# A tail of 232 matmuls in thirteen forms and 29 VectorE and GpSimd operations, added behind the output of a two-layer decoder

## The chip, the cores and the metric

The kernel runs on one NeuronCore of a Trainium2 chip. The metric is the device time of one execution in microseconds (us). Names of engines are those of the profile: PE is TensorE's matmul stream, PEld its weight loads, DVE is VectorE, ACT is ScalarE, POOL is GpSimd, SP is SyncE, which issues the loads.

## The reference

Two layers are applied to a residual `h` of 256 tokens by 1024 channels. All arithmetic is float32, and the output is the last residual.

```python
for i in range(DEPTH):                       # DEPTH = 2
    xn = rms_norm(h, norm_mix[i])
    u = xn @ w_in[i]                         # split into the inputs of four mixers
    branches = (o_a, o_b, o_c, o_d)          # RG-LRU, conformer, differential, sparse attention
    mixed = sum(sigmoid(xn @ w_gate[i, j]) * (branches[j] @ w_branch[i, j]) for j in range(4))
    h = h + mixed @ w_out[i]
    f = causal_dwconv(rms_norm(h, norm_ffn[i]) @ w_up[i], conv_f_w[i], conv_f_b[i])
    f_gate, f_val = jnp.split(f, 2, axis=-1)
    h = h + (jax.nn.silu(f_gate) * f_val) @ w_down[i]
    e = rms_norm(p[i] @ w_ple_in[i], ple_norm[i])
    g = sigmoid(rms_norm(h, ple_gate_norm[i]) @ w_ple_gate[i])
    h = h + g * e
return h
```

## The kernel before

The channels lie in the partitions and the tokens in the columns. The residual is four tiles `h[0]` to `h[3]` of 128 by 512 (two blocks of 128 channels, 256 tokens each). The weights come as a stream of pieces of 128 by 1024 float32. `prep_one` (line 205) loads a piece into `raw`, ACT writes its high part `hi` (line 214, type float32r) and DVE the remainder `lo` (line 215). A product is three matmuls on such parts, in `mm3` (lines 248 to 250): high by high, high by low, low by high. A matmul there takes 128 rows of contraction, a stationary operand of 128 columns and a moving operand of 256 columns. `tok_unit` (lines 476 to 478) does the same with moving operands of 512 columns. Side computations of the mixers use plain float32 matmuls: the RG-LRU gates at lines 794 and 796 (128 rows, 256 columns), the scores of the differential attention at line 703 (64 rows, because a head has 64 channels), each followed by a bfloat16 matmul on 128 rows at line 704 that adds the mask, and the sums of squares at line 271, with a moving operand of one column. In the trace a float32 matmul leaves two records on PE, one of float32r or bfloat16 a single record.

Each engine runs its instructions in the order of its own queue, and semaphores order them between engines. That order comes from a scheduler that follows the program and the dependences of the tiles. Tiles come from pools with a fixed number of buffers: `big` (38), `raw` (5), `hi` (6) and, in PSUM, `mm` and `sp` (4 banks each; `smbank` gives one `sp` bank).

The program ends with the last layer's gate. For each `h[i]`, PE computes the gate's product, DVE scales it (line 1038), ACT takes the tanh (line 1039), DVE multiplies and adds (lines 1040 and 1041), and ACT issues the DMA of that part of `h[i]` to the output (line 1043). `h[3]` is done in two halves of 256 columns. POOL does nothing but four memsets at the program's start.

Of the kernel before, what the change touches and what calls it, by code (L numbers as in the profile page):

```python
# [10 lines left out]
F32 = mybir.dt.float32  # L11
F32R = mybir.dt.float32r
# [6 lines left out]
P = 128  # L19
# [8 lines left out]
NEG = -1e30  # L28
THETA = 500000.0
PIECE = 1024  # L30
EARLY = 4  # feed-forward banks computed before the mean square is known
MIX = (0, 3, 2, 1)
MIX_ORDER = (("gate", MIX[0]), ("gate", MIX[1]), ("branch", MIX[0]), ("gate", MIX[2]), ("branch", MIX[1]),
             ("gate", MIX[3]), ("branch", MIX[2]), ("branch", MIX[3]))
# how far apart the steps of the side computations lie between the products: RG-LRU, conformer,
# differential attention, sparse attention, first half of the conformer's taps
EVERY = {0: 4.8, 1: 5.1, 2: 3.3, 3: 2.9, 4: 5.5}

# columns of the channel vectors
_V = {}  # L40
_o = 0
for _n, _w in (("norm_mix", 8), ("norm_ffn", 8), ("ple_gate_norm", 8), ("ple_norm", 8), ("conv_a_w", 16),
# [3 lines left out]
    _o += _w  # L46
NV = _o

# columns of the row vectors
_R = {}  # L50
_o = 0
for _n, _w in (("diff_q_norm", 64), ("diff_k_norm", 64), ("diff_lq1", 64), ("diff_lk1", 64), ("diff_lq2", 64),
# [2 lines left out]
    _o += _w  # L55
NR = _o

# columns of the shape-only constants
_C = {}
_o = 0  # L60
for _n, _w in (("ident", 128), ("nc30", 128), ("nc38", 128), ("rope_c", 64), ("rope_s", 128), ("rope_i", 32), ("hmask", 4)):
# [3 lines left out]


def unit_list(l):
    """One layer's weights in the order of their use: (key, source, pieces), a piece being
    (first k-tile, k-tiles, column ranges or counts of zero columns)."""
    u = []  # L70

    def tok(key, c0, c1, src="w_in", kt=KD):
        g = PIECE // (c1 - c0)
        u.append((key, src, [(k, g, [(c0, c1)]) for k in range(0, kt, g)]))

    def chan(key, src, c0, kt=KD, g=8):
        u.append((key, src, [(k, min(g, kt - k), [(c0, c0 + P)]) for k in range(0, kt, g)]))

    def bu(n):
        chan(("bv", n), "w_in", 1024 + n * P)  # L80
        chan(("bg", n), "w_in", 1536 + n * P)

    ple_in = [(("ple_in", i), "w_ple_in", [(0, 2, [(512 * i, 512 * i + 512)])]) for i in range(2)]
    if l:
        u.append(ple_in[0])
    for n in range(4):
        bu(n)
    if not l:
        u.append(ple_in[0])
    tok(("tok", "dq"), 3584, 4096)  # L90
    tok(("tok", "dk"), 4096, 4608)
    u.append((("ik", 0), "w_in", [(0, KD, [(4608, 4648), P - 40])]))
    tok(("tok", "cq"), 2048, 2560)
    tok(("tok", "ck"), 2560, 3072)
    tok(("tok", "cv"), 3072, 3584)
    for n in range(8):
        chan(("a", n), "w_in", n * P)
    for kind, j in MIX_ORDER:
        if kind == "gate":
            for n in range(8):  # L100
                chan(("gate", j, n), ("w_gate", j), n * P)
        else:
            for n in range(0, 8, 2):
                tok(("branch", j, n), n * P, (n + 2) * P, ("w_branch", j), 4)
    u.append(ple_in[1])
    for n in range(8):
        chan(("out", n), "w_out", n * P)
    for g in range(NG):
        chan(("upg", g), "w_up", g * P)
        chan(("upv", g), "w_up", D_FF + g * P)  # L110
    for n in range(8):
        chan(("down", n), "w_down", n * P, NG)
    for n in range(8):
        chan(("pg", n), "w_ple_gate", n * P)
    return u
# [7 lines left out]
def decoder_kernel(ctx: ExitStack, tc: tile.TileContext, w_dram, x_dram, p_dram, vec_dram, row_dram, lru_dram,  # L123
# [28 lines left out]
        return ps.tile([P, 4, P], F32, name=nm("sp"), tag="sp", bufs=4)  # L152

    def score_banks(Kw):
        """Banks for four maps [P, Kw]: (maps of the bank, bank [P, maps, Kw])."""
        n = 2 * S // Kw
        return [(range(i, i + n), smbank().rearrange("p a b -> p (a b)").rearrange("p (a b) -> p a b", a=n))
                for i in range(0, 4, n)]

# [1 line left out]
    h = [cst.tile([P, 2, S], F32, name=f"h{i}", tag=f"h{i}") for i in range(4)]  # L161
    con = cst.tile([P, NC], F32, name="con", tag="con")
    vec = [cst.tile([P, NV], F32, name=f"vec{l}", tag=f"vec{l}") for l in range(L)]
# [16 lines left out]
    mask_bf = cst.tile([P, 2, P], BF16, name="mask_bf", tag="mask_bf")  # L180
    ident_bf, nc30_bf = mask_bf[:, 0, :], mask_bf[:, 1, :]

    # the tensor engine's clock rises with activity: keep it busy until the first operands are there
    warm = smbank()
    for _ in range(12):
        T.matmul(warm[:, 0, :], ones, ones, start=True, stop=True)

# [1 line left out]
    stream = []  # L189
    pidx = 0  # L190
    for l in range(L):
# [34 lines left out]
        used[0] += npieces  # L226
        return r

# [1 line left out]
    def split(dst, src, scale=1.0):  # L230
        """dst = (hi, lo) from src, exactly."""
        hi, lo = dst
        if scale == 1.0:
            A.activation(hi, src, AF.Copy)  # L234
            V.tensor_tensor(lo, src, hi.bitcast(F32), op=ALU.subtract)  # L235
        else:
            A.activation(hi, src, AF.Copy, scale=scale)
            V.scalar_tensor_tensor(lo, src, scale, hi.bitcast(F32), op0=ALU.mult, op1=ALU.subtract)

    def mm3(out, wl, xs, c0, first, last):  # L240
        """out += W[:, c0:c0+128].T @ x over the piece's k-tiles."""
        wh, wlo = wl
        nk = len(xs)
        for k in range(nk):
            xh, xl = xs[k]
            a = wh[:, k, c0:c0 + P]
            b = wlo[:, k, c0:c0 + P]
            T.matmul(out, a, xh, start=first and k == 0, stop=False)  # L248
            T.matmul(out, a, xl, start=False, stop=False)  # L249
            T.matmul(out, b, xh, start=False, stop=last and k == nk - 1)  # L250
# [13 lines left out]
        V.tensor_tensor(acc[:, 0, :], acc[:, 0, :], acc[:, 1, :], op=ALU.add)  # L264

    def rnorm(acc, scale, bias):
        """1 / sqrt(scale * (sum over the channels) + bias) per token: with the tokens in
        partitions [P, 2], and in every partition [P, S]."""
        t = smbank()
        for b in range(2):  # L270
            T.matmul(t[:, 0, b:b + 1], acc[:, 0, b * P:(b + 1) * P], ones[:, 0:1], start=True, stop=True)  # L271
        rt = st([P, 2], "rt", 4)
        A.activation(rt, t[:, 0, 0:2], AF.Sqrt, scale=scale, bias=bias)
        V.reciprocal(rt, rt)
        t = smbank()
        for b in range(2):
            T.matmul(t[:, b, :], rt[:, b:b + 1].to_broadcast([P, P]), ident, start=True, stop=True)  # L277
        rs = st([P, S], "rs", 3)
        A.activation(rs, t[:, 0:2, :].rearrange("p a b -> p (a b)"), AF.Copy)
        return rt, rs  # L280

    class Norm:
        """RMSNorm over all channels of [128, 2, S] pairs. xs: split x * gain, for products whose
        result is scaled by r afterwards; xn(): split x * gain * r."""

        def __init__(self, gain, late=False):
            self.gain, self.late, self.pairs, self.xs, self.acc, self.squares = gain, late, [], [], None, 0
# [46 lines left out]
            return t  # L334

    def rope(t, H, W, tab, b):
        """t [128, H, W]: rotates the first W/4 columns of each head."""
        rot = W // 4
        half = rot // 2
        q = t[:, :, 0:rot]  # L340
        cs = tab[:, b, 0, :][:, None, :].to_broadcast([P, H, rot])
        sn = tab[:, b, 1, :]
        t1 = st([P, P], "rp1", 2)[:, :H * rot].rearrange("p (h r) -> p h r", h=H)
        t2 = st([P, P], "rp2", 2)[:, :H * rot].rearrange("p (h r) -> p h r", h=H)
        V.tensor_tensor(t1, q, cs, op=ALU.mult)
        V.tensor_tensor(t2[:, :, 0:half], q[:, :, half:rot], sn[:, None, 0:half].to_broadcast([P, H, half]), op=ALU.mult)
        V.tensor_tensor(t2[:, :, half:rot], q[:, :, 0:half], sn[:, None, half:rot].to_broadcast([P, H, half]), op=ALU.mult)
        V.tensor_tensor(q, t1, t2, op=ALU.add)
# [5 lines left out]
        split(hl, pT)  # L354
        return hl

    # ================= layers =================
    for l in range(L):
        vv = vec[l]
        rr = cst.tile([P, NR], F32, name=nm("row"), tag="row")  # L360
# [7 lines left out]
            o, w = _R[name]  # L368
            return rr[:, o:o + w]

# [1 line left out]
        if l == 0:  # L372
            nxt_nrm = Norm(vcol("norm_mix"), late=True)
            for i in range(4):
# [29 lines left out]

        if l:
            embed(0)
# [1 line left out]
        nrm = nxt_nrm  # L408
        xsk = ktiles(nrm.xs)
        bbanks = []  # L410
# [16 lines left out]
            A.activation(ident_bf, ident, AF.Copy)  # L427
            A.activation(nc30_bf, nc30, AF.Copy)

# [1 line left out]
        sv = st([P, 44], "sv", 2)  # L431
        hbr, hbi, lc2, lc4, b2 = (sv[:, 4 * i:4 * i + 4] for i in range(5))
        z, z2, pz, ee = (sv[:, 20 + 4 * i:24 + 4 * i] for i in range(4))
# [29 lines left out]
        hr = nrm.rt  # L463

        def tok_unit(xk, n, npieces):
            """u[:, cols] token-major, one bank per token block."""
            pcs = take(npieces)
            outs = []
            outs = [mmbank().rearrange("p a b -> p (a b)")[:, :n] for b in range(2)]
# [11 lines left out]
            return outs  # L481

        def weave(gens):
            """The steps of the generators in turn."""
            live = list(gens)
            while live:
                for g in list(live):
                    if next(g, "end") == "end":
                        live.remove(g)
                    else:  # L490
                        yield
# [11 lines left out]

        o_pairs = {}

# [1 line left out]
        def side_d():  # L507
            dq, dk, ik = raws["dq"], raws["dk"], raws["ik"]
            ms = st([P, 2, 6], "msd", 1)
# [142 lines left out]

            yield from weave(attend(b) for b in range(2))

# [1 line left out]
        def side_c():  # L656
            cq, ck, cv = raws["cq"], raws["ck"], raws["cv"]
            ms = st([P, 2, 2, 8], "msc", 1)
# [103 lines left out]
                                           op1=ALU.subtract)  # L762
                yield

# [1 line left out]
        xa, ga = [], []  # L766

        def evac_a(bank, i):
# [48 lines left out]
                oa.append(hl)  # L817
                yield

# [1 line left out]
        ypad = st([P, 4, S + 30], "ypad", 1)  # L821
        V.memset(ypad[:, :, 0:30], 0.0)

# [62 lines left out]
                for _ in sides.pop(k)[0]:  # L886
                    pass

# [1 line left out]
        for c in range(4):  # L890
            evac_b(nrm.scaled(bbanks[c]), c)
        if not l:
# [29 lines left out]
                fn(bank, i)  # L922
        side(0, side_a(), EVERY[0])

# [1 line left out]
        mixed = {}  # L926
        gates = {}
        ms_ = []
# [41 lines left out]
            V.scalar_tensor_tensor(h[i], bank, 0.5, h[i], op0=ALU.mult, op1=ALU.add)  # L970
            nrm.add(h[i])

# [1 line left out]
        _, rs = rnorm(acc[0], 4.0 / D, eps[:, 1:2])  # L974
        for i in range(4):
            V.tensor_tensor(e[i], e[i], rs[:, None, :].to_broadcast([P, 2, S]), op=ALU.mult)
# [70 lines left out]
                nxt_nrm.add(h[i])  # L1047


def _rope_rows(head_dim):  # L1050
    rot = head_dim // 4
    inv = np.float32(THETA) ** (-np.arange(0, rot, 2, dtype=np.float32) / np.float32(rot))
# [18 lines left out]


def _chan(a):
    """[C] or [taps, C] -> [128, C/128 * taps]: channel c*128+p at partition p."""
    a = np.asarray(a)
    if a.ndim == 1:
        a = a[None]
# [51 lines left out]
```

## Time and profile before

| | |
|---|---|
| time, median of two runs | 1067.38 us (1066.74 and 1068.01) |
| span of the profiled execution, first to last instruction | 1064.7 us |
| PE busy | 1056.7 us, 99% of the span |
| DVE, ACT busy | 874.1 us, 708.1 us |
| POOL busy | 0.2 us |
| HBM read | 181.21 MB, 171 GB/s over the span |

The page gives the span of the profiled execution and not its time; the two times shown are 2.0 and 3.3 us longer than the span, the median 2.7 us. A busy share says how much of the span an engine had an instruction in hand. Matmuls overlap in the array, so a matmul's price is read from the distance between the starts of two neighbours and not from its length.

### The profile page before, as it was taken

What the parts mean: (1) busy time and instruction counts of PE and PEld (TensorE: products, weight loads), DVE (VectorE), ACT (ScalarE), POOL (GpSimd) and SP (SyncE); (2) the same over time, 40 slices, a digit from 0 to 9 for tenths busy, and PEclk for the clock granted to TensorE, in tenths of its full rate; (3) what the DMA queues carried; (4) which work ended last, traced back from release to release, by engine and by line L of the source; (5) the groups of instructions that cost most, each with busy time, mean ns of one, the idle gap of its engine ahead of it and who ended that gap; (6) DMA issues with size and microseconds to landing.
All of it is one profiled execution on the core that took longest, in us unless ns stands there. A gap on an engine that the chain in (4) does not pass through costs nothing.

```text
span 1064.7 us, 20765 instructions
## 1 busy us (share of the span) xinstructions
PE 1056.7 (99%) x8168; PEld 1018.3 (96%) x8168; DVE 874.1 (82%) x1629; ACT 708.1 (67%) x1207; POOL 0.2 (0%) x4
## 2 busy tenths in 40 slices
PE   8999999999999999999999999999999999999998
PEld 8888999899999999999998899998999999999998
DVE  7999999868888997855787899997779789877554
ACT  7876788668466766544677769876685667665442
POOL 0000000000000000000000000000000000000000
PEclk9999999999999999999999999999999999999999
DMA  8755244434555365555554643443455554655541
GB/s 299 279 188 194 100 142 166 159 131 158 190 182 175 121 237 183 179 188 194 181 187 167 214 163 120 139 171 115 165 169 185 173 181 147 221 177 176 184 161 40
DMA packets 52369, 183.60 MB, mean 172 GB/s; under 512 B 5808, under 2 KB 6320, under 8 KB 52272
## 3 DMA queue, kind: packets, MB, share of 16 engines
q1 hardware_dynamic: 51408, 181.05, 49.9%
q8 instruction: 64, 1.05, 0.4%
q10 hardware_dynamic: 864, 1.24, 0.4%
q14 instruction: 33, 0.27, 0.1%
HBM read 181.21 MB, written 1.05 MB: 171 GB/s over the span
## 4 chain that ended last, share of the span: by engine, by line
PE 98%; DVE 1%; DMA 0%; ACT 0%; issue 0%; DVEq 0%
PE mm L249 27%; PE mm L248 27%; PE mm L250 27%; PE mm L476 3%; PE mm L478 3%; PE mm L477 3%; PE sp L703 2%; PE sp L564 1%; PE sp L625 1%; PE sp L733 1%; PE sp L704 0%; PE sp L648 0%; DMA vec<-in_vec_dram 0%; PE sp L277 0%; PE sp L271 0%; PE sp L683 0%
## 5 line engine op out<-in xcount | busy, mean ns | idle before, releaser
L248 PE MATMUL mm<-b,hi 128*128 128x256 f32 x2384 | 680.5, 286 | 1.9 <-ACT hi L214 1.7
L250 PE MATMUL mm<-b,lo 128*128 128x256 f32 x2384 | 675.6, 284 | 0.2 <-DVE lo L215 0.2
L249 PE MATMUL mm<-b,hi 128*128 128x256 f32 x2384 | 675.8, 284 | 0.0
L214 ACT ACTIVATE hi<-raw 128x1024 fp32r<-128x1024 f32 (+1 forms) x343 | 357.2, 1046 | 259.0 <-PE mm L249 199.0
L215 DVE TENSOR_TENSOR lo<-raw,hi 128x1024 fp32r<-128x1024 f32 (+1 forms) x343 | 411.1, 1204 | 122.8 <-ACT hi L214 120.1
L248 PEld LDWEIGHTS mm<-b,hi 128*128 128x128 f32 x2384 | 457.4, 192 | 3.0 <-ACT hi L214 1.9
L249 PEld LDWEIGHTS mm<-b,hi 128*128 128x128 f32 x2384 | 458.0, 192 | 1.3 <-issue 0.5
L250 PEld LDWEIGHTS mm<-b,lo 128*128 128x128 f32 x2384 | 457.8, 192 | 0.4 <-DVE lo L215 0.4
L840 DVE SCALAR_TENSOR_TENSOR b<-s,vec,b 128x256 f32<-128x256 f32 x240 | 103.6, 476 | 0.0
L476 PE MATMUL mm<-hi,b 128*128 128x512 f32 x160 | 62.9, 393 | 0.0
L478 PE MATMUL mm<-hi,b 128*128 128x512 f32 x160 | 62.5, 390 | 0.0
L477 PE MATMUL mm<-lo,b 128*128 128x512 f32 x160 | 62.4, 390 | 0.0
L1009 DVE SCALAR_TENSOR_TENSOR s<-mm,vec,s 128x255 f32<-128x255 f32 (+1 forms) x144 | 59.8, 474 | 1.7 <-ACT s L1003 1.7
L234 ACT ACTIVATE b<-b 128x512 fp32r<-128x512 f32 x56 | 35.0, 628 | 28.1 <-DVE b L1013 18.4
L235 DVE TENSOR_TENSOR b<-b,b 128x512 fp32r<-128x512 f32 x56 | 38.4, 686 | 12.3 <-ACT b L234 12.3
L478 PEld LDWEIGHTS mm<-hi,b 128*128 128x128 f32 x160 | 30.0, 188 | 6.4
L476 PEld LDWEIGHTS mm<-hi,b 128*128 128x128 f32 x160 | 30.0, 188 | 6.4
L1003 ACT ACTIVATE s<-mm,vec 128x256 f32<-128x256 f32 x72 | 36.1, 551 | 0.0
L477 PEld LDWEIGHTS mm<-lo,b 128*128 128x128 f32 x160 | 30.1, 188 | 5.8
L709 ACT ACTIVATE s<-sp,s,s 128x128 f32<-128x128 f32 (+1 forms) x32 | 16.0, 507 | 12.7 <-DVE s L706 12.7
L295 ACT ACTIVATE b<-h,vec 128x256 fp32r<-128x256 f32 x48 | 21.4, 497 | 2.4 <-DVE h L1041 2.4
L296 DVE SCALAR_TENSOR_TENSOR b<-h,vec,b 128x256 fp32r<-128x256 f32 x48 | 20.8, 478 | 0.8 <-ACT b L295 0.8
(206 smaller groups left out, 792.4 us busy)
## 6 DMA issues: line engine op xcount, KB each, us to landing
raw<-in_w_dram SPq DMA_DIRECT2D x325, 512.0 KB, 3.3
raw<-in_w_dram SPq DMA_DIRECT2D x16, 384.0 KB, 2.9
h<-in_x_dram SPq DMA_DIRECT2D x4, 256.0 KB, 5.1
b<-in_lru_dram SPq DMA_DIRECT2D x4, 256.0 KB, 6.1
out_dram<-h ACTq DMA_DIRECT2D x3, 256.0 KB, 2.5
row<-in_row_dram SPq DMA_DIRECT2D x2, 336.0 KB, 5.6
raw<-in_w_dram SPq DMA_DIRECT2D x2, 256.0 KB, 5.0
b<-in_p_dram SPq DMA_DIRECT2D x2, 256.0 KB, 4.9
```

Of the source, the lines that this page charges most:

```text
L214: A.activation(hi[:, cs], raw[:, cs], AF.Copy)
L215: last_lo[0] = V.tensor_tensor(lo[:, cs], raw[:, cs], hi[:, cs].bitcast(F32), op=ALU.subtract).ins
L235: V.tensor_tensor(lo, src, hi.bitcast(F32), op=ALU.subtract)
L248: T.matmul(out, a, xh, start=first and k == 0, stop=False)
L249: T.matmul(out, a, xl, start=False, stop=False)
L250: T.matmul(out, b, xh, start=False, stop=last and k == nk - 1)
L476: T.matmul(outs[b], xk[k][0][:, bs], wh[:, kk, :], start=k == 0, stop=False)
L477: T.matmul(outs[b], xk[k][0][:, bs], wl[:, kk, :], start=False, stop=False)
L478: T.matmul(outs[b], xk[k][1][:, bs], wh[:, kk, :], start=False, stop=k == last)
L840: V.scalar_tensor_tensor(t, ypad[:, c, d:d + S], w[:, 31 * c + d:31 * c + d + 1], t, op0=ALU.mult, op1=ALU.add)
L1003: A.activation(cf[:, 2 * q + s_, :], bank[:, s_, :], AF.Identity, scale=w[:, 3 * c + 2:3 * c + 3], bias=bb[:, c:c + 1])
L1009: V.scalar_tensor_tensor(t, bank[:, s_, :S - d], w[:, 3 * c + 2 - d:3 * c + 3 - d], t, op0=ALU.mult, op1=ALU.add)
```

## The change

Code is added at the end of `decoder_kernel`, after the loop over the layers. ACT copies `h[0]` to `wide` and `h[3]` to `stat` (both float32r) and `h[3]` to `wbf` (bfloat16). Thirteen calls of `run` then issue 232 matmuls into `sp` banks that nothing reads. `full` uses all 128 rows (or 96 of the stationary columns); `rows` takes 64 or 32 rows at a time, from the partitions of one row group after the other, and writes each row group to its own bank. Beside it ACT copies `h[2]` and `h[3]` into one tile `src` of 128 by 1024, and a chain of 15 DVE and 14 POOL operations of 128 by 1024 runs on it, handing tiles back and forth. No result of the tail goes to the output, and no instruction of the kernel before is taken out. The other changed lines of the diff are comments and docstrings.

```diff
@@ -1047,6 +1047,77 @@
                 nxt_nrm.add(h[i])


+    wide = big.tile([P, 2, S], F32R, name=nm("b"), tag="big", bufs=NBIG)
+    A.activation(wide, h[0], AF.Copy)
+    stat = big.tile([P, 2, S], F32R, name=nm("b"), tag="big", bufs=NBIG)
+    A.activation(stat, h[3], AF.Copy)
+    w32, x32, idn = h[3], h[0], ident
+    wbf = cst.tile([P, 2, S], BF16, name="wbf", tag="wbf")
+    A.activation(wbf, h[3], AF.Copy)
+
+    def flat(bank):
+        return bank.rearrange("p a b -> p (a b)")
+
+    def run(n, make):
+        banks = [smbank() for _ in range(4)]
+        for q in range(n):
+            make(q, [flat(b) for b in banks])
+
+    def full(w, x, N, M=P):
+        def f(q, banks):
+            T.matmul(banks[q % 2][:M, :N], w[:, q % 2, 0:M], x.rearrange("p a b -> p (a b)")[:, :N], start=True, stop=True)
+        return f
+
+    def rows(w, x, N, k):
+        n = P // k
+        def f(q, banks):
+            r = q % n
+            rs = slice(r * k, (r + 1) * k)
+            T.matmul(banks[r][:, :N], w[rs, (q // n) % 2, 0:P], x.rearrange("p a b -> p (a b)")[rs, :N], start=True, stop=True)
+        return f
+
+    run(16, full(stat, wide, 256))
+    run(16, rows(stat, wide, 256, 64))
+    run(16, full(stat, wide, 256))
+    run(32, rows(stat, wide, 256, 32))
+    run(16, full(stat, wide, 512))
+    run(16, rows(stat, wide, 512, 64))
+    run(16, full(stat, wide, 128))
+    run(16, full(stat, wide, 256, 96))
+    run(16, full(wbf, wbf, 256))
+    run(16, rows(wbf, wbf, 256, 64))
+    run(8, full(w32, x32, 256))
+    run(16, rows(w32, x32, 256, 64))
+    run(32, rows(w32, x32, 256, 32))
+
+    src = wp.tile([P, PIECE], F32, name=nm("raw"), tag="raw", bufs=RAW_BUFS)
+    for i in range(2):
+        A.activation(src[:, 512 * i:512 * i + 512].rearrange("p (a b) -> p a b", a=2), h[2 + i], AF.Copy)
+    G = nc.gpsimd
+
+    def tmp(dtype=F32):
+        return wp.tile([P, PIECE], dtype, name=nm("hi"), tag="hi", bufs=SPLIT_BUFS)
+
+    hi = tmp(F32R)
+    V.tensor_copy(hi, src)
+    d = [tmp(F32R) for _ in range(2)]
+    for q in range(2):
+        V.tensor_tensor(d[q], src, hi.bitcast(F32), op=ALU.subtract)
+    g = [tmp(F32R) for _ in range(2)]
+    for q in range(2):
+        G.tensor_tensor(g[q], d[q].bitcast(F32), hi.bitcast(F32), op=ALU.subtract)
+    for q in range(6):
+        V.tensor_tensor(d[q % 2], g[0].bitcast(F32), hi.bitcast(F32), op=ALU.subtract)
+        G.tensor_tensor(g[1], g[0].bitcast(F32), hi.bitcast(F32), op=ALU.subtract)
+    for q in range(3):
+        V.tensor_copy(d[q % 2], g[1].bitcast(F32))
+    for q in range(3):
+        G.tensor_copy(g[0], d[q % 2].bitcast(F32))
+    for q in range(3):
+        V.scalar_tensor_tensor(d[q % 2], g[0].bitcast(F32), 1.0, hi.bitcast(F32), op0=ALU.mult, op1=ALU.subtract)
+        G.tensor_tensor(g[1], g[0].bitcast(F32), hi.bitcast(F32), op=ALU.subtract)
+
+
 def _rope_rows(head_dim):
     rot = head_dim // 4
     inv = np.float32(THETA) ** (-np.arange(0, rot, 2, dtype=np.float32) / np.float32(rot))
```


On ACT, at the program's end, two of the tail's copies are put between the steps of the last gate (`raw` is the tile `src`, `b_13147` is `wide`), and three behind the last output DMA (`b_13149` is `stat`):

```order
 L1043 DMA out_dram<-h_72 128x512
 L1039 ACTIVATE b_13110<-b_13110 128x256
+L1095 ACTIVATE raw_13437<-h_72 128x512
 L1043 DMA out_dram<-h_73 128x256
+L1051 ACTIVATE b_13147<-h_70 128x512
 L1039 ACTIVATE b_13141<-b_13141 128x256
 L1043 DMA out_dram<-h_73 128x256
-L1124 UNCONDITIONAL_BRANCH
+L1053 ACTIVATE b_13149<-h_73 128x512
+L1056 ACTIVATE wbf<-h_73 128x512
+L1095 ACTIVATE raw_13437<-h_73 128x512
```

The copies of `h[2]` and `h[0]` now stand ahead of the last two output DMAs' steps, the copies of `h[3]` behind them.

On POOL, whose rows ended with the branch after the memsets, this stands behind that branch now (`hi_13440` is `hi`, 13442 and 13443 are `d[0]` and `d[1]`, 13446 and 13447 `g[0]` and `g[1]`):

```order
 L1108 ISA
 L1108 TENSOR_TENSOR hi_13446<-hi_13442,hi_13440 128x1024
 L1108 TENSOR_TENSOR hi_13447<-hi_13443,hi_13440 128x1024
 L1111 TENSOR_TENSOR hi_13447<-hi_13446,hi_13440 128x1024 x6
 L1115 CAST hi_13446<-hi_13442 128x1024
 L1115 CAST hi_13446<-hi_13443 128x1024
 L1115 CAST hi_13446<-hi_13442 128x1024
 L1118 TENSOR_TENSOR hi_13447<-hi_13446,hi_13440 128x1024 x3
```

POOL waits there for DVE's `d[0]` and `d[1]`, and DVE's subtractions at line 1110 and casts at line 1113 wait for POOL's results; nothing moved on POOL, all of it is new.

## Rows read from the trace of the kernel before

**Rows 1.** the page: busy time, share of the span, instructions; then the chain's engines

```profile
PE 1056.7 (99%) x8168; PEld 1018.3 (96%) x8168; DVE 874.1 (82%) x1629; ACT 708.1 (67%) x1207; POOL 0.2 (0%) x4
...
PE 98%; DVE 1%; DMA 0%; ACT 0%; issue 0%; DVEq 0%
```

**Rows 2.** timeline of the end: start us, us, engine, line, operation [idle, releaser]

```profile
1059.58 0.28 PE L250 MATMUL mm<-b,lo 128*128 128x256 f32 x1
1059.90 0.42 DVE L1038 TENSOR_TENSOR b<-mm,s 128x256 f32<-128x256 f32 x1 [1.08 <-PE mm L250]
1060.36 0.42 ACT L1039 ACTIVATE b<-b 128x256 f32<-128x256 f32 x1 [2.46 <-DVE b L1038]
...
1061.26 0.42 DVE L1041 TENSOR_TENSOR h<-b,h 128x256 f32<-128x256 f32 x1
1061.72 0.34 ACTq L1043 DMA_DIRECT2D out_dram<-h  x1
```

**Rows 3.** DMA issues of the page: KB each, us from issue to landing

```profile
out_dram<-h ACTq DMA_DIRECT2D x3, 256.0 KB, 2.5
```

**Rows 4.** groups by line and form: xcount, busy us, mean ns, idle us

```profile
L215 DVE TENSOR_TENSOR lo<-raw,hi 128x1024 fp32r<-128x1024 f32 x325 | 394.5, 1219 | 116.4 <-ACT hi L214 114.2
...
L234 ACT ACTIVATE b<-b 128x512 fp32r<-128x512 f32 x56 | 35.0, 628 | 28.1 <-DVE b L1013 18.4 <-DVE b L814 4.0 <-DVE b L955 3.2
...
L812 DVE TENSOR_TENSOR_SCAN b<-b,b 128x256 f32<-128x256 f32 x8 | 5.0, 668 | 0.0
...
L1040 DVE SCALAR_TENSOR_TENSOR b<-b,b 128x512 f32<-128x512 f32 x7 | 4.8, 688 | 2.8 <-ACT b L1039 2.8
...
L348 DVE TENSOR_TENSOR b<-s,s 128x128 f32<-128x128 f32 x12 | 3.4, 281 | 0.0
...
L535 DVE COPY s<-s 128x128 f32<-128x128 f32 x4 | 0.9, 213 | 0.0
```

**Rows 5.** the same view for POOL alone, first of four like rows

```profile
L1117 POOL MEMSET const-bfloat16-1.0<- 128x1 bf16 x1 | 0.1, 101 | 0.0
```

**Rows 6.** timeline of PE, 512-column matmuls of one token unit

```profile
36.58 0.40 PE L476 MATMUL mm<-hi,b 128*128 128x512 f32 x1
36.81 0.40 PE L477 MATMUL mm<-lo,b 128*128 128x512 f32 x1
```

**Rows 7.** chain in order of time: start us, us, what (two float32 matmuls)

```profile
129.59 0.87 PE sp L794 x4
```

**Rows 8.** timeline of PE's weight loads around four one-column matmuls

```profile
1039.87 0.53 PEld L271 LDWEIGHTS sp<-ones,b 128*128 128x128 f32 x4
1040.33 0.19 PEld L249 LDWEIGHTS mm<-b,hi 128*128 128x128 f32 x1
```

**Rows 9.** timeline of PE: float32 on 64 rows beside bfloat16 on 128

```profile
157.39 0.28 PE L249 MATMUL mm<-b,hi 128*128 128x256 f32 x1
157.51 0.28 PE L250 MATMUL mm<-b,lo 128*128 128x256 f32 x1
157.72 0.48 PE L703 MATMUL sp<-b,b 64*128 64x128 f32 x2
158.14 0.23 PE L704 MATMUL sp<-mask_bf 128*128 128x128 bf16 x1
```

**Rows 10.** stretches: busy of PE, PEld, DVE, ACT, POOL; then PEclk, DMA, GB/s

```profile
6.00:7.00 1.00, 0.00 (x0) 0.00 (x0) 1.00 (x3) 1.00 (x3) 0.00 (x0) 1.00 1.07 389
...
9.00:10.00 1.00, 1.00 (x7) 1.00 (x6) 1.00 (x3) 1.00 (x4) 0.00 (x0) 0.50 1.05 428
12.00:14.00 2.00, 2.00 (x19) 2.00 (x18) 1.93 (x5) 1.97 (x6) 0.00 (x0) 0.97 1.03 411
1063.20:1063.40 0.20, 0.00 (x0) 0.00 (x0) 0.00 (x0) 0.00 (x0) 0.00 (x0) 1.00 0.00 0
1063.60:1064.00 0.40, 0.00 (x0) 0.00 (x0) 0.00 (x0) 0.00 (x0) 0.00 (x0) 0.50 0.00 0
```

## The prediction

> **What bounds the kernel now.** I read the page first: PE is busy 99% of the span and makes 98% of the chain that ended last, and POOL is busy 0.2 us [rows 1]. So the kernel is one PE stream, and whatever is put behind it has nothing to hide under, except the few microseconds after the last matmul. These I read from the timeline of the end: the last matmul starts at 1059.58, the last addition to `h[3]` (line 1041) ends at 1061.68, and the last output DMA is issued from 1061.72 to 1062.06 [rows 2]. With 2.5 us to landing [rows 3] the output is complete at about 1064.2 to 1064.6, which is the span of 1064.7. The median time is 2.7 us longer than that span, and I carry these 2.7 us over.
>
> **What starts when.** Nothing is removed, and no step of the old program is put behind an added one for long: two copies of 128 by 512 stand between the last steps on ACT, at 0.63 us each [rows 4]. ACT idles 2.46 us before its last tanh at 1060.36 [rows 2], which covers both copies and the DMA issue between them; uncovered they would cost at most 1.3 us. All the rest needs `h[3]`, which is final at 1061.68. Behind the DMA issue ACT writes `stat` from 1062.06 to 1062.69, then `wbf`, then the second half of `src` until 1062.06 + 3 x 0.63 = 1063.95. Two chains start there and run side by side: PE's from about 1062.8, DVE and POOL's from 1063.95. The later one sets the end. The output's landing, at 1064.6, is hidden under both.
>
> **PE's chain.** The price of a matmul is the distance between starts. For float32r with 256 columns it is 0.12 us [rows 9], with 512 columns 0.23 [rows 6]. A float32 matmul of 128 rows and 256 columns costs 0.87 / 2 = 0.435 (four records are two matmuls) [rows 7]. With one column, four records are still (1040.33 - 1039.87) / 4 = 0.115 apart [rows 8], so a weight load of 128 columns takes about 0.11 however short the matmul is. I take 0.11 for float32r with 128 columns (0.23 as the upper end, the price of four times the columns), and 0.12 for 96 stationary columns and for bfloat16, whose rows never stand side by side in the trace. The forms on all rows: 48 x 0.12 = 5.8 (two calls of 256 columns and the one with 96), 16 x 0.23 = 3.7, 16 x 0.11 = 1.8, bfloat16 16 x 0.12 = 1.9, float32 8 x 0.435 = 3.5; together 16.7 us.
>
> The forms on 64 or 32 rows are the open price. The trace has float32 on 64 rows, but two records of one row group and then a matmul on 128 rows [rows 9]; row groups in turn, as the tail has them, it does not show. Upper bound: each costs what the full form costs, 16 x 0.12 + 32 x 0.12 + 16 x 0.23 + 16 x 0.12 + 16 x 0.435 + 32 x 0.435 = 32.2 us. Lower bound: two row groups run at once for 64 rows and four for 32, which leaves 11.7 us. In between, the multiplications overlap and the weight loads do not; then a record costs no less than 0.11, and the sum is 1.8 + 3.5 + 1.8 + 1.8 + 3.5 + 7.0 = 19.4 us. Ten times the form changes between 128, 64 and 32 rows. At such a place the next record starts 0.21 behind the one before and the one after that 0.42 behind a pair [rows 9], 0.1 to 0.3 more than in a stream; I take 0.2, 2.0 us in all. PE ends at 1062.8 + 16.7 + 2.0 + 32.2 + 0.3 (the last one's length) = 1114.0 without overlap, at 1093.5 with all of it, at 1101.2 with loads alone in turn.
>
> **DVE and POOL's chain.** A DVE subtraction of 128 by 1024 takes 1.22 us (line 215), and `SCALAR_TENSOR_TENSOR` has the same rate: 0.69 for 512 columns [rows 4]. From 281 ns for 128 columns and 1219 for 1024, a two-operand operation costs 1.05 ns per column and 147 ns fixed. The copy of line 535 takes 213 ns for 128 columns, 0.52 per column, so a DVE cast of 1024 is about 0.68 us (1.22 as upper end). POOL has four memsets of one column at 0.1 us [rows 5] and no operation on two tiles. Its lower bound is DVE's 1.22; the upper is the slowest two-operand row, the scan of line 812 at 668 / 256 = 2.6 ns per column, 2.67 us. The copy at half the price per column says that operands read are what is paid for. If POOL reads one operand after the other it needs two passes, 2 x 1.22 = 2.44, which is also near the scan; I take that, and one pass, 1.22, for a POOL cast.
>
> The two engines wait for each other at four places: POOL's first subtraction for `d[0]`, DVE's six subtractions of line 1110 for `g[0]`, DVE's casts of line 1113 for POOL's last subtraction of line 1111, and POOL's casts for DVE's. What may overlap is `d[1]` with POOL's first, the six subtractions with POOL's seven, and the last three with the last three: ten DVE operations, 12.2 us. Whether two engines that read two operands each get in each other's way is not in the trace, as POOL stands idle in it; the bound is 0 to 12.2. I take all of it, since the reads are what each pays for. In turns: 1063.95 + 0.68 + 2 x 1.22 + 11 x 2.44 (POOL) + 6 x 1.22 + 3 x 0.68 + 3 x 1.22 (POOL casts) + 3 x 1.22 = 1110.6, and some 20 handovers at 0.04 (line 1041's end to the DMA issue [rows 2]) make it 1111.4. Side by side it is 1099.2. What speaks for turns from outside this trace is the Trainium skill, SBUF — State Buffer, section SBUF: two separate sides: VectorE and GpSimd share a port pair that one instruction holds whole while the other blocks, also when VectorE reads two SBUF operands. No run here shows it; by it the sum is the 1111.4 above. The skill's GPSIMD Engine Reference, section Performance versus the Vector engine, has 4497 ns for 2048 columns on GpSimd; as an estimate that is 2.25 us for 1024, and the chain would end 2.1 us earlier.
>
> **The sum.** With PE's row groups overlapped, DVE and POOL end last, at 1111.4 plus some 0.2 for the final barrier: 47 us over the old span of 1064.7, so 1067.4 + 47 = 1114 us.
>
> **The rivals.** First, **row groups one after the other**: PE ends at 1114.0 and the time is 1117. For it speaks that float32 on 64 rows shows no discount, two records of 128 columns in 0.48 [rows 9]; against it, that those two are of one row group. The skill's TensorEngine Tiling (Array Packing), section Key Properties, says that different tiles load and multiply in parallel and that a change of mode drains the array; the 0.21 at the change agrees, the rest no row shows.
>
> Second, **short chains**: row groups overlap and POOL runs beside DVE. Then PE ends at 1101.2 (loads in turn) and POOL at 1099.2; the time is 1102 to 1104, or 1098 if POOL is as quick as 2.0.
>
> Third, **the lower clock**. PE's granted clock stood at half, 1.2 GHz, from 9 to 10 us after a stretch in which PE did nothing from 6 to 7, and was back at 2.4 GHz from about 12; at the end it fell between 1063.4 and 1063.6, 3.6 us after the last matmul [rows 10]. The tail's first matmul comes 2.9 us after it, so the clock may fall there as well and cost some 1.7 us, half of a stretch as long as the one from 9 to 12. This is inside the range. If the narrow forms keep the clock at half for good, the 20.9 us of float32 on 64 and 32 rows double and the time is about 1138.
>
> Fourth, **no cost**, the other side: 232 matmuls that nothing reads lie behind the last DMA issue. If the time were taken when the output has landed, the tail would be outside of it and the time would stay at 1067. It decides only if the measured time ends with the output and not with the last engine; the added instructions are in the built program, and the time exceeds the whole span, which speaks against it.
>
> **How the numbers follow.** Turns with overlapped row groups 0.41, row groups one after the other 0.30, short chains 0.22, lower clock for good 0.04, no cost 0.03. The forecast is 1114; POOL's price between 2.0 and 2.67 moves it from 1109 to 1117. The low end of 1102 takes in most of the short chains, the high end of 1120 the serial rows with a stretch at half clock. Two per cent, about what a measurement of this kernel can tell from no change, is 21 us: only the last case stays below it, so slower has 0.97.
>
> **What would show it.** In the changed kernel's profile the old program must end as before, with the last output DMA issued at about 1061.7. PE should then be busy to between 1093 and 1102, with starts in `rows` closer than 0.12 (float32r) and 0.2 (float32); starts at 0.12 and 0.21 there mean no overlap. POOL's 14 operations should start 2.4 us apart where DVE is idle and about 3.7 apart beside DVE's subtractions; 2.4 throughout means no turns. A PEclk below 1.00 after 1063 shows the third rival. The prediction is wrong if POOL's operations cost more than 2.67, if the waits between runs of matmuls drain PE for more than 0.3 us each, or if POOL needs long before its first operation.

## The result, and the profile after

The changed kernel takes 1109.43 us (median of two runs, 1109.36 to 1109.50) against 1067.38 before: 42 us longer, a ratio of 1.0393 with a 95% interval of 1.0374 to 1.0413. Its profiled execution took 1109.5 us with a span of 1107.7.

The page of the changed kernel, sections 1 and 4, shows where the new work is. POOL has 38.0 us, and the chain that ended last, 98% PE in [rows 1], now has POOL in it, at its end:

```profile
PE 1088.7 (98%) x8456; PEld 1045.7 (94%) x8456; DVE 907.3 (82%) x1644; ACT 711.1 (64%) x1212; POOL 38.0 (3%) x18
...
PE 95%; POOL 3%; DVE 1%; DMA 0%; ACT 0%; issue 0%; POOLq 0%; ACTq 0%; DVEq 0%
```

The timeline of the changed kernel around the end of the old program (start us, us, engine, line, operation) is the counterpart of [rows 2]:

```profile
1061.54 0.42 DVE L1041 TENSOR_TENSOR h<-b,h 128x256 f32<-128x256 f32 x1
1061.99 0.34 ACTq L1043 DMA_DIRECT2D out_dram<-h  x1
1062.38 0.63 ACT L1053 ACTIVATE b<-h 128x512 fp32r<-128x512 f32 x1 [1.33 <-DVE h L1041]
...
1063.43 0.62 ACT L1095 ACTIVATE raw<-h 128x512 f32<-128x512 f32 x1
...
1064.08 0.69 DVE L1102 CAST hi<-raw 128x1024 fp32r<-128x1024 f32 x1 [2.12 <-ACT raw L1095]
...
1066.21 3.21 POOL L1108 TENSOR_TENSOR hi<-hi,hi 128x1024 fp32r<-128x1024 f32 x1 [1065.77 <-PE sp L1068]
```

The old program ends as before: `h[3]` is final at 1061.54 + 0.42 = 1061.96 (1061.68 in [rows 2], where the output DMA was issued at 1061.72). Behind the DMA issue ACT's three copies run from 1062.38 to 1064.05, DVE starts its chain at 1064.08 and POOL at 1066.21. POOL's row names a matmul of line 1068 as what released it. But POOL starts 1.40 us after DVE's first subtraction (1064.81 in this trace), and it starts 1.40 us after it without the matmuls too (1066.09 and 1067.49 in the trace of the first experiment): what it waits for is `d[0]`.

The tail's groups by line and form in the changed kernel (xcount, busy us, mean ns, idle before):

```profile
L1110 DVE TENSOR_TENSOR hi<-hi,hi 128x1024 fp32r<-128x1024 f32 x6 | 19.9, 3388 | 2.3 <-POOL hi L1108 2.3
L1111 POOL TENSOR_TENSOR hi<-hi,hi 128x1024 fp32r<-128x1024 f32 x6 | 19.4, 3229 | 0.5
L1118 POOL TENSOR_TENSOR hi<-hi,hi 128x1024 fp32r<-128x1024 f32 x3 | 9.8, 3259 | 0.2
...
L1117 DVE SCALAR_TENSOR_TENSOR hi<-hi,hi 128x1024 fp32r<-128x1024 f32 x3 | 7.8, 2647 | 3.4 <-POOL hi L1115 3.4
L1115 POOL CAST hi<-hi 128x1024 fp32r<-128x1024 f32 x3 | 3.1, 1041 | 2.2 <-DVE hi L1113 2.1
```

A DVE subtraction of 128 by 1024, 1219 ns in [rows 4], shows 3388 ns beside POOL. Six of them take 19.9 us, as long as POOL's six, 19.4. Neither engine idles in between (0.5 us), so these lengths seem to be mostly waits inside an instruction, which the experiments with other DVE operations test. The chain of the changed kernel in order of time (start us, us, what) gives the rhythm:

```profile
1071.85 3.27 POOL hi L1111
...
1075.18 3.26 POOL hi L1111
...
1088.40 3.22 POOL hi L1111
...
1091.64 1.91 DVE hi L1113 x3
...
1093.67 1.05 POOL hi L1115
...
1097.01 3.38 POOL hi L1118
...
1100.46 3.20 POOL hi L1118
...
1103.70 3.24 POOLq L1195
```

From 1071.85 to 1075.18, and on average until 1091.62, a step takes 3.3 us: six steps, 19.8 us. POOL's casts start 1.1 us apart. The last POOL subtraction, which the chain has under POOL's final drain, ends at 1106.94, and the span ends 0.8 us later.

PE's timeline of the changed kernel, equal records merged:

```profile
1063.06 3.11 PE L1068 MATMUL sp<-b,b 128*128 128x256 f32 x16 [2.93 <-ACT b L1053]
1066.10 1.74 PE L1076 MATMUL sp<-b,b 64*128 64x256 f32 x16
1067.77 2.18 PE L1068 MATMUL sp<-b,b 128*128 128x256 f32 x16
1069.88 1.34 PE L1076 MATMUL sp<-b,b 32*128 32x256 f32 x32
...
1075.02 2.12 PE L1076 MATMUL sp<-b,b 64*128 64x512 f32 x16
...
1087.27 7.53 PE L1076 MATMUL sp<-h,h 64*128 64x256 f32 x96
```

A row's length is from the first start to the last end. 16 matmuls of 512 columns on 64 rows take 2.12 us: with the last one's 0.39 taken off, 15 steps of 0.115, half of the 0.23 in [rows 6]. 32 matmuls of 256 columns on 32 rows take 1.34 us, 0.034 each, a little over a quarter of the 0.12 in [rows 9]. The last row holds 32 float32 records on 64 rows and 64 on 32 rows: 7.53 us where full price would be 20.9. PE ends at 1094.80, 12 us before POOL.

Stretches of the changed kernel (busy of PE, PEld, DVE, ACT, POOL; then PEclk, DMA share, GB/s) show the granted clock:

```profile
1062.00:1063.90 1.90, 0.84 (x7) 0.84 (x8) 0.00 (x0) 1.52 (x3) 0.00 (x0) 1.00 0.20 69
1064.00:1067.00 3.00, 3.00 (x19) 2.77 (x19) 2.88 (x3) 0.05 (x1) 0.79 (x1) 0.50 0.00 0
1068.00:1090.00 22.00, 22.00 (x186) 18.49 (x187) 19.95 (x6) 0.00 (x0) 21.53 (x8) 1.00 0.01 1
1091.00:1094.80 3.80, 3.80 (x64) 3.40 (x64) 1.90 (x3) 0.00 (x0) 1.67 (x3) 1.00 0.00 0
```

From 1064 to 1067 the clock stood at 0.50, 1.2 GHz, after PE had idled from the old program's last matmul to 1063.06, 2.9 us. That is why the first two rows of the PE timeline, 3.11 and 1.74 us, are longer than their like would need: in an execution that kept the clock at 1.00 they take 2.18 and 1.21 (rows of such a one stand with the run in which DVE copies). Later it is 1.00, narrow matmuls included.

### The profile page after: what moved, and what is told of

Read it like the earlier page. It is cut to its first block, busy times and chain, and to the rows that moved or that the text cites. A ratio compares the mean times of both kernels' runs of the same rounds, so it can differ in the third digit from the quotient of the medians.

```text
span 1107.7 us, 21385 instructions
## 1 busy us (share of the span) xinstructions
PE 1088.7 (98%) x8456; PEld 1045.7 (94%) x8456; DVE 907.3 (82%) x1644; ACT 711.1 (64%) x1212; POOL 38.0 (3%) x18
## 4 chain that ended last, share of the span: by engine, by line
PE 95%; POOL 3%; DVE 1%; DMA 0%; ACT 0%; issue 0%; POOLq 0%; ACTq 0%; DVEq 0%
PE mm L249 26%; PE mm L248 26%; PE mm L250 26%; PE mm L476 3%; PE mm L478 3%; PE mm L477 3%; POOL hi L1111 2%; PE sp L703 2%; PE sp L564 1%; POOL hi L1118 1%; PE sp L625 1%; PE sp L733 0%; PE sp L704 0%; PE sp L648 0%; DMA vec<-in_vec_dram 0%; PE sp L277 0%
## 5 line engine op out<-in xcount | busy, mean ns | idle before, releaser
L1108 POOL TENSOR_TENSOR hi<-hi,hi 128x1024 fp32r<-128x1024 f32 x2 | 5.6, 2803 | 1065.8 <-PE sp L1068 1065.8
L709 ACT ACTIVATE s<-sp,s,s 128x128 f32<-128x128 f32 (+1 forms) x32 | 16.0, 509 | 12.7 <-DVE s L706 12.7
```

## The experiments

The theory after the result: the DVE and POOL chain alone sets the end, because the two engines take turns where both read two operands; PE's tail lies beside it. The rivals: PE's stream slows the chain down; POOL's subtraction simply costs 3.3 us; narrow matmuls overlap whatever rows they use. Eight kernels ran. Times are medians, in three rounds beside the kernel before, which had a median of 1068.26 us beside the first four and 1067.10 beside the last four.

### The chain without the matmuls

```diff
-    run(16, full(stat, wide, 256))
...
-    run(32, rows(w32, x32, 256, 32))
```

> Leaves out the 232 added matmuls and keeps the copies on ACT and the chain of DVE and POOL. Theory (that chain alone sets the end, and PE's work lies beside it for nothing): the last POOL subtraction ends at about 1106.9 as in the changed kernel, the time stays at 1109.4 within 1 us, and POOL's starts stay 3.3 us apart beside DVE. Rival (PE's stream makes POOL and DVE slower): POOL's subtractions go back towards 2.4 us and the time falls by 3 us or more.

Measured: 1109.27 us, ratio 1.0389 (1.0373 to 1.0405), the changed kernel's time. POOL's six subtractions by line and form:

```profile
L1097 POOL TENSOR_TENSOR hi<-hi,hi 128x1024 fp32r<-128x1024 f32 x6 | 19.2, 3201 | 0.5
```

3201 ns against 3229 with the matmuls. PE's 232 matmuls cost nothing here, and they slow POOL by no more than 0.03 us per operation.

### The matmuls without the chain

```diff
-    src = wp.tile([P, PIECE], F32, name=nm("raw"), tag="raw", bufs=RAW_BUFS)
...
-        G.tensor_tensor(g[1], g[0].bitcast(F32), hi.bitcast(F32), op=ALU.subtract)
```

> Leaves out the chain of DVE and POOL and the copies that feed it, and keeps the 232 matmuls. Theory: PE ends at 1094.8 as in the changed kernel and then sets the end; with 0.8 us from there to the end of the span and 1.8 us outside of it the time is 1097.3, 12 us less. Rival (the matmuls only look hidden, both chains hold each other up): PE ends clearly before 1094, and the time is under 1095.

Measured: 1096.75 us, ratio 1.0269 (1.0253 to 1.0286), 12.7 us less than the changed kernel. PE's timeline has nearly the same rows as there:

```profile
1063.06 2.94 PE L1068 MATMUL sp<-b,b 128*128 128x256 f32 x16 [2.93 <-ACT b L1053]
...
1087.28 7.53 PE L1076 MATMUL sp<-h,h 64*128 64x256 f32 x96
```

It ends at 1087.28 + 7.53 = 1094.81. So PE's end does not depend on the chain of DVE and POOL, and by the run before that chain hardly depends on PE. Of the four executions, two (1097.56, the profiled one, and 1097.28 us) have a mean granted clock of 0.997 and two (1096.22 and 1096.06) 1.000: the stretch at half clock at the tail's start does not come in every execution.

### DVE with one operand, summed

```diff
-        V.tensor_tensor(d[q % 2], g[0].bitcast(F32), hi.bitcast(F32), op=ALU.subtract)
+        V.tensor_reduce(red, g[0].bitcast(F32), axis=AX.X, op=ALU.add)
```

> The six DVE subtractions at line 1110 become six sums over the columns of one tile, so that DVE reads one operand there and not two; nothing else changes. Theory (POOL and a DVE operation with two operands take turns): POOL's six starts come 2.4 us apart and not 3.3, the chain ends 5 us earlier and the time is 1104. Rival (any DVE operation beside POOL takes turns with it): starts stay about 3.3 apart and the time stays at 1109.

Measured: 1105.05 us, ratio 1.0346 (1.0331 to 1.0362). The groups (POOL's line is one further down):

```profile
L1112 POOL TENSOR_TENSOR hi<-hi,hi 128x1024 fp32r<-128x1024 f32 x6 | 14.3, 2376 | 0.5
...
L1111 DVE TENSOR_REDUCE red<-hi 128x1 f32<-128x1024 f32 x6 | 7.3, 1220 | 2.5 <-POOL hi L1109 2.3
```

The first and the last of POOL's six in the chain, in order of time:

```profile
1071.74 2.41 POOL hi L1112
...
1084.05 2.36 POOL hi L1112
```

POOL's subtraction is down to 2376 ns, its starts are (1084.05 - 1071.74) / 5 = 2.46 us apart, and DVE's sum takes its own 1220 ns beside it. Once `g[0]` is there the sums run one behind the other and are through by 1076.84; POOL's starts are 2.48 apart beside them and 2.45 behind them. So 3.3 us is not POOL's price, and being busy at the same time is not what makes them wait.

### DVE with one operand, copied

```diff
-        V.tensor_tensor(d[q % 2], g[0].bitcast(F32), hi.bitcast(F32), op=ALU.subtract)
+        V.tensor_copy(d[q % 2], g[0].bitcast(F32))
```

> The six DVE subtractions at line 1110 become six copies of one tile by DVE (one operand read, a whole tile written at the fast rate of 0.69 us). Theory A (only a second operand read makes DVE and POOL take turns): POOL's six starts come 2.4 to 2.5 us apart as beside the sums, and the time is 1105. Theory B (a copy at the fast rate takes a turn too): the starts come 2.15 + 0.6 = 2.8 us apart, and the time is 1106 to 1107. Rival (turns with anything, at the old price): 3.3 apart and 1109.

Measured: 1106.24 us, ratio 1.0370 (1.0355 to 1.0386). The groups, and the first and the last of POOL's six in the chain:

```profile
L1110 DVE CAST hi<-hi 128x1024 fp32r<-128x1024 f32 x6 | 16.7, 2820 | 2.4 <-POOL hi L1108 2.3
L1111 POOL TENSOR_TENSOR hi<-hi,hi 128x1024 fp32r<-128x1024 f32 x6 | 16.2, 2696 | 0.5
...
1071.76 2.74 POOL hi L1111
...
1085.65 2.69 POOL hi L1111
```

A copy that needs 0.69 us alone shows 2820 ns, and POOL's subtraction 2696. POOL's starts lie (1085.65 - 1071.76) / 5 = 2.78 us apart, as theory B has it: the fast copy takes turns with POOL although it reads one operand. The sum, which also reads one operand but takes 1220 ns for it, does not. The two differ in their rate and in what they write, a whole tile or one column; no run has a slow operation with one operand that writes a whole tile, so which of the two makes the copy take turns is not shown.

The three kernels give the price of a pair. POOL's starts are 2.46 us apart beside the sums, 2.78 beside the copies and (1088.40 - 1071.85) / 5 = 3.31 beside the subtractions. So a copy of 0.69 us adds 0.32, and a subtraction of 1.22 adds 0.85: in both, about 0.37 us of DVE's operation costs POOL nothing.

PE's rows of this trace and its stretch behind the gap, where the clock did not fall:

```profile
1062.97 2.18 PE L1068 MATMUL sp<-b,b 128*128 128x256 f32 x16 [2.93 <-ACT b L1053]
1065.08 1.21 PE L1076 MATMUL sp<-b,b 64*128 64x256 f32 x16
...
1064.00:1067.00 3.00, 3.00 (x32) 2.73 (x31) 2.97 (x3) 0.00 (x0) 0.87 (x1) 1.00 0.00 0
```

With the same idle gap of 2.93 us ahead of it, PE's tail ran at full clock here. It ends at 1093.25, 30.3 us after its start, where the changed kernel's took 31.7: the half clock at the tail's start costs 1.5 us.

### All narrow matmuls in one row group

```diff
-            rs = slice(r * k, (r + 1) * k)
+            rs = slice(0, k)
```

> Every matmul on 64 or 32 rows takes the first row group and not one after the other; counts, shapes and banks stay. Theory (row groups overlap because they are different): all of them now go one after the other, PE gains 20 us and ends at about 1115, past POOL's 1106.9, and the time is about 1118. Rival (narrow matmuls overlap, whatever their row group): PE ends at 1095 and the time stays at 1109.

Measured: 1131.55 us, ratio 1.0606 (1.0569 to 1.0644), 14 us more than the theory's 1118. PE's timeline in the profiled execution, which took 1127.73 us:

```profile
1066.18 2.17 PE L1076 MATMUL sp<-b,b 64*128 64x256 f32 x16
...
1070.38 4.08 PE L1076 MATMUL sp<-b,b 32*128 32x256 f32 x32
...
1078.25 3.94 PE L1076 MATMUL sp<-b,b 64*128 64x512 f32 x16
...
1093.20 31.84 PE L1076 MATMUL sp<-h,h 64*128 64x256 f32 x96
```

On 64 rows 16 float32r matmuls now take 2.17 us, 0.126 a step, and 32 on 32 rows 4.08, 0.123 a step: the overlap is gone, and the full price of the prediction's upper bound is right. The 10 us that this execution took over the theory's 1118 are in the last row, 31.84 us where 20.9 was expected, and the stretches say why:

```profile
1093.00:1100.00 7.00, 7.00 (x34) 5.90 (x32) 3.59 (x3) 0.00 (x0) 6.37 (x4) 1.00 0.00 0
1100.00:1103.00 3.00, 3.00 (x15) 2.33 (x14) 3.00 (x2) 0.00 (x0) 2.92 (x2) 1.00 0.00 0
1104.00:1124.00 20.00, 20.00 (x49) 15.60 (x48) 0.50 (x1) 0.00 (x0) 2.70 (x1) 0.50 0.00 0
```

With PE busy all the time, the clock stands at 1.00 to 1103 and at 0.50 from 1104, in the float32 matmuls on one group of 32 rows. The four executions took 1127.7 and 1128.3 us at a mean granted clock of 0.987, and 1134.8 and 1135.2 at 0.980; where the clock fell in the longer two no trace shows.

### The last run on 64 rows, one row group

The chain of DVE and POOL is left out.

```diff
-            rs = slice(r * k, (r + 1) * k)
+            rs = slice(0, k)
...
-    run(32, rows(w32, x32, 256, 32))
+    run(32, rows(w32, x32, 256, 64))
```

> Matmuls only (the chain of DVE and POOL is left out), narrow matmuls in the first row group as in the fourth run, and the last 32 float32 matmuls take 64 rows in place of 32. Theory (a single group of 32 rows in use is too little for the full clock, 64 rows are enough): PEclk stays 1.00 in the last 14 us, starts are 0.215 apart, PE ends near 1114 and the time is 1117. Rival (the clock falls behind any long serial stretch of narrow float32 matmuls): PEclk falls to 0.50 and the time is 1124 or more.

Measured: 1120.3 us, ratio 1.0518 (1.0480 to 1.0556). In the profiled execution the clock stayed full for all 96 records:

```profile
1093.00:1114.00 21.00, 21.00 (x98) 17.87 (x96) 0.00 (x0) 0.00 (x0) 0.00 (x0) 1.00 0.00 0
```

But the four executions split: 1116.8 (the profiled one) and 1117.3 us with a mean clock of 0.997, as the theory has it, and 1123.3 and 1126.1 with 0.991 and 0.988. In these two the clock was at half for longer, and they have no trace: that it fell in the last run is likely but not shown, since the kernel's other narrow runs take one row group too. The theory holds for two executions of four.

### Only the last run on one group of 32 rows

The chain of DVE and POOL is left out.

```diff
-    run(32, rows(w32, x32, 256, 32))
+    run(32, rows(w32, x32, 256, 32, 1))
...
-    def rows(w, x, N, k):
+    def rows(w, x, N, k, groups=4):
...
-            rs = slice(r * k, (r + 1) * k)
+            g0 = r % groups
+            rs = slice(g0 * k, (g0 + 1) * k)
```

> Matmuls only (the chain of DVE and POOL is left out), row groups in turn as in the changed kernel except in the last run of 32 float32 matmuls on 32 rows, which all take the first row group. Theory (32 rows alone drop the clock, without DVE or POOL having a part in it): starts are 0.215 apart for about 3 us, then 0.43, PE ends near 1114 to 1117 and the time is 1116 to 1119. Rival (the drop in the fourth run came with the other engines' work or the long serial stretch before it): the clock stays full, PE ends at 1105 and the time is 1107.5.

Measured: 1118.27 us, ratio 1.0479 (1.0463 to 1.0494), and all four executions between 1117.0 and 1118.6. The stretches:

```profile
1091.00:1094.00 3.00, 3.00 (x15) 2.49 (x14) 0.00 (x0) 0.00 (x0) 0.00 (x0) 1.00 0.00 0
1096.00:1115.00 19.00, 19.00 (x46) 14.88 (x45) 0.00 (x0) 0.00 (x0) 0.00 (x0) 0.50 0.00 0
```

The clock fell again, between 1094 and 1096, with DVE and POOL idle and with no run on a single row group before the last one. The same 64 records in four row groups run at 1.00 in the changed kernel's stretch from 1091. But there they are done in some 4 us, and here the records on one row group also ran at 1.00 for their first 3 us: whether a longer stretch in four row groups would keep the clock was not tried.

### No gap before the tail

The chain of DVE and POOL is left out.

```diff
+    keep = smbank()
+    for _ in range(16):
+        T.matmul(keep[:, 0, :], ones, ones, start=True, stop=True)
     run(16, full(stat, wide, 256))
```

> Matmuls only, as in the second run (the chain of DVE and POOL is left out), with 16 float32 matmuls of 128 columns on constants put between the last product and the first added matmul, 3.4 us of PE's work where it idled 3.2. Theory (the idle gap dropped PE's clock to 1.2 GHz for 3 us at the tail's start): PEclk stays 1.00 and the added matmuls come 0.12 us apart from the first; they start up to 0.5 later but end 1 us earlier, and the time is 1095.5 to 1096.5. Rival (the slow start belongs to the tail's own first matmuls): starts stay 0.21 apart for 3 us and the time is 1097 or more.

Measured: 1097.29 us, ratio 1.0283 (1.0268 to 1.0298), against 1096.75 without the filler. By the times this is inconclusive: the run of the kernel before varies by 1.5 us in the same rounds (1066.33 to 1067.86), as much as was to be shown. PE's timeline and the stretches:

```profile
1064.61 2.16 PE L1068 MATMUL sp<-b,b 128*128 128x256 f32 x16
1066.69 1.21 PE L1076 MATMUL sp<-b,b 64*128 64x256 f32 x16
...
1087.34 7.53 PE L1076 MATMUL sp<-h,h 64*128 64x256 f32 x96
```

```profile
1061.00:1064.00 3.00, 3.00 (x29) 3.00 (x28) 1.27 (x3) 1.17 (x3) 0.00 (x0) 1.00 0.13 45
1064.00:1067.00 3.00, 3.00 (x28) 2.87 (x28) 0.00 (x0) 0.68 (x2) 0.00 (x0) 1.00 0.12 42
```

The clock stays at 1.00, the first 16 matmuls take 2.16 us in place of 2.94 in the second run, and the next 16 take 1.21 in place of 1.93. From the first added matmul to PE's end it is 1064.61 to 1094.87, 30.3 us, against 1063.06 to 1094.81, 31.8. But the filler delays the first added matmul, which now comes 1.51 us after `h[3]` is final (1063.10 in that trace) and not 1.10, and that execution's old program ended 1.1 us later.

The trace does not decide for the theory either, because the clock also stayed at 1.00 in profiled executions without filler. Seven traces have the tail's matmuls behind an idle gap of 2.93 us. In four the clock fell at the tail's start (the changed kernel, the second run, the sums, all narrow matmuls in one row group); in three it did not, and the first 16 matmuls took 2.18 us (the copies, the last run on 64 rows, only the last run on one group). This excludes the rival, that the tail's own first matmuls are slow. That the gap is what lets the clock fall fits the four, but whether the filler prevents it is not shown, and what decides between the four and the three is open.

## Why the prediction was right

The forecast was 1114 us in 1102 to 1120, with DVE and POOL taking turns beside a PE chain whose row groups overlap. The time was 1109.4, and this case is the one that came, to which the prediction gave 0.41.

**What ends last.** POOL ends at 1106.9 and PE at 1094.8. Shown by taking away the one (1109.3 without the matmuls) and the other (1096.8 without the chain).

**Turns.** The bound was 0 to 12.2 us and the forecast took the upper end. A step of POOL is 2.46 us beside the sums and 3.31 beside DVE's subtractions, 0.85 more and not 1.22. Over ten pairs that is 8.5 us in place of 12.2. The reason that the prediction gave, two engines that read two operands each, is only part of it: a copy that reads one operand takes a turn as well. The Trainium skill's SBUF — State Buffer, section SBUF: two separate sides, has the exclusive lock with this condition, two SBUF operands or a two-port mode; that the subtractions (3.31 us a step) and the copies (2.78) take turns and the sums do not agrees with it. That section of the Trainium skill has the lock held for the whole instruction; the measured step is shorter, 3.31 us where 2.46 and 1.22 make 3.68. The traces show the waits, not the port itself.

**POOL's price.** 2.44 was taken for a subtraction, 2.38 measured (2.46 from start to start); 1.22 for a cast, 1.04 measured (1.10 from start to start). No row showed POOL at such work, and that it needs a second pass over the operands is not shown by any run: the number came out close, which is in part luck. The estimate of 2.25 from the Trainium skill's GPSIMD Engine Reference, section Performance versus the Vector engine, was 0.13 low.

**PE.** The lower bound, 1093.5, was right but for the clock: 1094.8. It has PE's tail at 30.7 us, and at full clock it took 30.3. Row groups in turn overlap fully, also in their weight loads (0.034 us a record on 32 rows, where 0.11 was the price of a load), so the middle price of 19.4 us is excluded. With one row group all of it goes at full price. A change of form costs less than the 0.2 us that were taken: with the copies the last matmul of the first run starts at 1062.97 + 2.18 - 0.28 = 1064.87 and the next one, on 64 rows, 0.21 later, 0.09 more than in a stream. The half clock at the tail's start, named as the third rival, came for about 3 us and cost 1.5 where 1.7 was priced (half of the 3 us from 9 to 12 would have been 1.5), hidden under POOL.

**Where the 5 us are.** The sum put the chain's end at 1111.4, and it came at 1106.9. The six steps of line 1111 took 19.8 us where 6 x (2.44 + 1.22) = 22.0 was reckoned; the last three 9.9 for 11.0; the casts of both engines about 5.4 for 5.7; the rest is in the first pair and the handovers. The term that was mis-sized is the turn, a step of 3.3 us in place of 3.66. The large errors went the same way, too long, so the forecast was not right by errors that cancel. Around it the end of the span took 0.8 and not 0.2, and 1.8 us lay outside of the span and not 2.7: the 2.7 was a median set against the span of one execution.

**The rivals.** Row groups one after the other, priced at 1117, are excluded by the starts. Short chains are excluded by the 3.3 us steps. No cost is excluded by the 42 us: the time runs to the last engine, whether or not anything reads its result. The clock for good did not come in the changed kernel. A fall like it came in the runs with the narrow matmuls in one row group, at 1127.7 to 1135.2 us, below the rival's 1138: in the trace, about 20 us of the last row stand at half clock and the rest at full.

## What to carry to other kernels

Work that nothing reads still counts to the last engine's end, so a tail of measurements must be priced chain by chain and the longer one taken. Matmuls on 64 or 32 rows were cheap here only where successive ones used different row groups; in one group they cost the full price, and in long float32 runs the clock fell as well. Before GpSimd is put beside VectorE, see what VectorE runs there: beside GpSimd's subtractions a two-operand operation or a fast copy made both wait, a sum over the columns did not.

## What the runs showed of the hardware that was not expected

PE's granted clock fell to 1.2 GHz although PE had no gap, when its matmuls were float32 on a single group of 32 rows. The trace of the last experiment but one shows it: 46 records in the 19 us at half clock, 0.41 us each, against 15 in 3 us before the fall, 0.2 each. The other three executions of that kernel have no trace, but the same time within 1.6 us and mean clocks of 0.987 to 0.990. On a single group of 64 rows the profiled execution kept 2.4 GHz for all 21 us, and two executions of four were 6 to 9 us longer at a lower mean clock; what decides that is open. In four row groups in turn the same records kept 2.4 GHz, for the 4 us that they took; so did 32 float32r matmuls on the single group of 32 rows, for their 4.08 us. Whether the type, the row group or the length of the run decides is not separated by these runs.

A VectorE copy shows 2.8 us in the trace where 0.69 is its work: beside POOL an instruction's length holds its wait, so the price of a pair is read from starts. So read, a pair costs about 0.37 us less than the sum of the two, for the copy and for the subtraction alike.
